# Second FFN's output kept in rows with the residual turned back to rows beforehand; attention with three PSUM banks for transposes, one bank for two accumulators, and one product for the learned tokens' values

## Chip, cores and metric

One core of one Trainium2 chip. The metric is device time in microseconds (us) of one execution. The kernel before takes 1973.4 us, the median of three runs (1972.02 to 1973.48). The engines are PE (TensorE matmul; PEld its weight loads), DVE (VectorE), ACT (ScalarE), POOL (GpSimd) and SP (SyncE, which issues most DMAs).

## What is computed

One layer of a decoder trunk on 1024 tokens of width 1024, with 16 learned tokens ahead of them, all in float32:

```python
h = h + 0.5 * swiglu(rms_norm(h, ffn1_norm), ffn1_w_in, ffn1_w_out)
u = rms_norm(h, mix_norm) @ w_in
hq, hf, hi, hg, sq, sk, sv = jnp.split(u, ...)
o_hg = hgrn2(hq, hf, hi, hg, lb, hgrn_out_norm, valid)     # gated recurrence, 4 heads
o_sb = stick_breaking(sq, sk, sv, sb_q_norm, sb_k_norm, valid)   # 8 heads of 64
h = h + concat([o_hg, o_sb]) @ w_out
h = h + 0.5 * swiglu(rms_norm(h, ffn2_norm), ffn2_w_in, ffn2_w_out)
return h[:, pad + N_META:, :]
```

`swiglu(h, w_in, w_out)` is `(silu(g) * u) @ w_out` with `g, u = split(h @ w_in)`; the inner width is 2816. In `stick_breaking` a query t weighs each earlier key s, the learned tokens among them, with `sigmoid(z_ts) * prod_{s<j<t} (1 - sigmoid(z_tj))`, and the output is the sum of weights times values.

## The kernel before

**Numbers.** Products are made of two parts of each float32 operand: a rounded high part (`wh`, `xh`, ...) and the rest (`wl`, `xl`, ...). Where three PE instructions stand together they are high by high, low by high and high by low. ACT casts the high part, DVE subtracts for the low one.

**Stages.** The first FFN runs to about 700 us; projections of queries, keys and values follow (to 870), then the attention (to 1141), the recurrence and the output projection of the mix (to 1324), and the second FFN: `fast_in` (its products with w_in, 1324 to 1748) and `fast_out` (with w_out, 1748 to the end). The activations lie transposed, features on partitions and tokens along a row (`hT`), in the FFNs.

**fast_out** multiplies 2x2 blocks in seven block products, named A12, A11, S1, S2, S4, S3, A22 after the left operand. Their sums are gathered in two groups of four PSUM banks, x and y. A finished group m is added with factor 0.5 onto the residual (`evict`, L703 on DVE). The residual `hT` was stored to DRAM as `h2D` ahead of `fast_in` and is loaded again in `fast_out` (L2347). After S3 and after A22 half of the tokens is done: `store_out` turns it back to rows, four transposes (L1065) to a bank, 32 transposes a call; ACT (L1068) or DVE (L1070) copies each bank to a row tile `orow`, and SP stores it (L1071).

**Attention.** 8 heads by 4 pairs of 128-query blocks make 32 jobs (`sb_jobs`). A job has three lists of steps: scores (`z`, L1624, L1625, L1627; ACT's sigmoids L1630 and L1631; a DVE scan L1634; POOL's product L1640), turns (the weights are transposed on PE into a bank `flip`, L1479, those of the learned tokens by L1533, and split by ACT, L1602, and DVE, L1603, to `wu` or `wm`), and values. A value step is a product with the high weights over 128 columns of v, which holds its high part in 64 columns and its low part in the other 64 (L1554), and one with the low weights over the high 64 (L1556). The last value step of a job is that of the learned tokens (`oacc<-wm,v`). Then `sb_out` copies the lower half of the accumulator (ACT, `olow`, L1595) and adds it to the upper half (DVE, `ot`, L1596).

**What sets the order.** PE's order is that of the program text (manual schedule). `braid` (L1681) lays the three lists of each job on a time grid, with lags of two jobs for the turns and three for the values, and fills in between with projections for the recurrence (`proj`, L258 to L260; their gates L1126, L1133, L1134, their weights' split L241 and L243). The other engines are ordered by a scheduler by what each instruction needs. SP issues its DMAs in queue order. PSUM has 8 banks: in the attention 2 for the fill's projections, 2 for scores (`pz`), 2 for flips (`ptr`) and 2 for accumulators (`po`, tiles `oacc`).

**Other lines of the change.** `put_split` of keys and queries (L1397) casts to `ohi`; the last of them is the kT piece of head pair 3. `fast_in` splits each weight block at L369 (ACT) and L371 (DVE), `s` being a sum of blocks made on POOL or DVE (L390) and `raw` a block as loaded; its products are `qa`, `qb`, `qc` (L458), read by DVE at L490, L541, L548 and L551. The function that turned x at the start of the kernel (L1047, tiles `xrow` and `xts`, DRAM `xD`) transposes 32x32 squares on DVE and lets the DMA place the squares.

Of the kernel before, what the change touches and what calls it, by code (L numbers as in the profile page):

```python
# [49 lines left out]
class Block:  # L50
# [308 lines left out]
    def fast_in(self, ops, n, w_in, actD, openers, ev0, open_ev, feed=None, meta=None, spare=None,  # L359
# [7 lines left out]
        def operand(src):  # L367
            hi = wp.tile([P, 4, P], F32R, tag="wh", name="wh", bufs=3)
            nc.scalar.copy(hi, src)  # L369
            lo = wp.tile([P, 4, P], F32R, tag="wl", name="wl", bufs=3)  # L370
            nc.vector.tensor_sub(lo, src, hi.bitcast(F32))  # L371
            return hi, lo
# [3 lines left out]
        def block(i, h, col):  # L376
            t = wp.tile([P, 4, P], F32, tag="raw", name="raw", bufs=self.in_bufs)
            with self.tc.issue_after(loaded[-1].ins) if loaded else ExitStack():
# [3 lines left out]
                ))  # L382
            return t
# [240 lines left out]
    def fast_out(self, hT, cs, n, w_out, actD, ready, between=lambda a, q: None,  # L624
                 meta=lambda a, q, blocks: None):
# [74 lines left out]
        def evict(bank, i, j, step, ms=range(4)):  # L700
            for m in ms:
                h = hT[:, 4 * i + m, cs[j] : cs[j] + n]
                nc.vector.scalar_tensor_tensor(  # L703
                    h, banks[bank][m], 0.5, h, ALU.mult, ALU.add
                )
            if 3 in ms:
                ready(step)
# [7 lines left out]
        for bank, a, b, start, (i, j) in steps:  # L715
# [4 lines left out]
            for q in range(nq):  # L720
# [10 lines left out]
                for m, e, at, wh, wl, xh, xl in order:  # L731
                    y, z = ((wh, xh), (wl, xh), (wh, xl))[e]
                    nc.tensor.matmul(  # L733
# [324 lines left out]
    def store_out(self, hT, pool, pps, c0, n, tag):  # L1058
        nc = self.nc
        for i, r0 in enumerate(range(c0, c0 + n, P)):  # L1060
            for q in range(2):
                row = pool.tile([P, 512], F32, tag="orow", name="orow", bufs=4)
                ps = pps.tile([P, 4, P], F32, tag=f"{tag}{(2 * i + q) % 4}", name="o")
                for k in range(4):
                    nc.tensor.transpose(ps[:, k, :], hT[:, 4 * q + k, r0 : r0 + P], self.ident)  # L1065
                dst = row.rearrange("p (k c) -> p k c", k=4)
                if q == 0:
                    nc.scalar.copy(dst, ps)  # L1068
                else:
                    nc.vector.tensor_copy(dst, ps)  # L1070
                nc.sync.dma_start(self.out[0, r0 : r0 + P, 512 * q : 512 * q + 512], row)  # L1071
# [30 lines left out]
    def hgrn_fill(self, xh, xl, pool, dst):  # L1102
# [3 lines left out]
        self.stores, self.level_banks = [], "zo"  # L1106
# [4 lines left out]
        def use(kind, h, ps, c0, n):  # L1111
# [11 lines left out]
            elif kind == "f":  # L1123
                k = staged(n)
                nc.scalar.activation(t, ps, AF.Sigmoid)
                nc.scalar.activation(k, ps, AF.Sigmoid, scale=-1.0)  # L1126
# [16 lines left out]
        def part(i, ci, c0, n, half):  # L1143
            if ci == 0 and half == 0:
                kept["w"] = self.ahead_w.pop(cols[i])
                for c in cols[i + 1 : i + (3 if i == 0 else 2)]:
# [260 lines left out]
    def sb_v(self, p, vT, mix, vD):  # L1407
# [6 lines left out]
        for c0, nb, m in ((META, 16, 32), (META + 512, 16, 32), (0, 1, META)):  # L1414
# [9 lines left out]
            for b in range(4):  # L1424
                to = vD[p, b // 2, :m, j0 : j0 + nb].rearrange(
                    "r j (i b d) -> r (j i) b d", i=2, b=2
                )
                with self.tc.issue_after(self.last_load.ins):
# [6 lines left out]
    def sb_qk(self, p, qT, kT, pool, mix, dst):  # L1435
# [31 lines left out]
        for src, c0, b0, nb in rows:  # L1467
# [4 lines left out]
            with self.tc.issue_after(self.rounds[self.columns[-1]]) if p == 3 else ExitStack():  # L1472
# [9 lines left out]
    def sb_jobs(self, keys, fetch, pool):  # L1482
# [29 lines left out]
        def job(p, hh, qs, ks, v, b0):  # L1512
# [15 lines left out]
            def meta():  # L1528
                wm.extend(kept["wm"][0])
# [4 lines left out]
                self.sb_parts([t[:META] for t in wm], ps)  # L1534
# [7 lines left out]
            def values(j):  # L1542
                if j == 0:
                    acc.append(self.po.tile([P, 256], F32, tag="o", name="oacc"))
                o = acc[0]
                if j == b0 + 2:
                    w = [t.rearrange("p b t -> p (b t)") for t in wm]
                    vj, c = v[:, 0], slice(0, 256)
                else:
# [4 lines left out]
                nc.tensor.matmul(o[:, c], vj, w[0], start=j == 0, stop=False,  # L1554
                                 skip_group_check=True)
                nc.tensor.matmul(o[:64, c], vj[:, :64], w[1], start=False, stop=end,  # L1556
                                 skip_group_check=True)
# [7 lines left out]
        kept["wm"] = [[fetch.tile([P, 2, P], F32R, name=f"wm{j}{i}") for i in range(2)]  # L1565
                      for j in range(2)]
        for t in chain(*kept["wm"]):
            nc.vector.memset(t.bitcast(F32), 0.0)
        none = kept["wm"][1][1].rearrange("p b t -> p (b t)").bitcast(F32)[META:]
        for p in range(4):  # L1570
            for a in range(4):
                to = vD[p, :, 0 if a else META :, a].rearrange("h r c -> r h c")
                nc.sync.dma_start(
                    to, none[: to.shape[0]].rearrange("r (h c) -> r h c", h=2)
# [186 lines left out]
    def run(self):  # L1761
# [21 lines left out]
        with ExitStack() as c0:  # L1783
            with ExitStack() as c1:
# [373 lines left out]
                with tc.manual_schedule(engines={nc.tensor.engine}):  # L2158
# [14 lines left out]
                    cf.close()  # L2173
                    self.proj_tags[0] = tag
# [24 lines left out]
            self.h2D = self.dram.tile([KT, P, SEQ], F32, name="h2D")  # L2199
            ph = self.pool("h2")  # L2200
# [12 lines left out]
            with tc.manual_schedule(engines={nc.tensor.engine}), ExitStack() as cx:  # L2213
# [96 lines left out]
                def after_opened():  # L2310
                    both = ph.tile([P, 16, n], F32R, tag="h2", name="parts", bufs=1)
                    self.parts = {"w": both[:, :8], "t": both[:, 8:]}

                steps = self.fast_in(
                    ops, n, a["ffn2_w_in"][0], actD, 2, ev0, open_ev, made,
                    after_opened=after_opened,
# [9 lines left out]
                drain(steps)  # L2326
            with tc.manual_schedule(engines={nc.tensor.engine}), ExitStack() as c1:
                self.ring = self.pool("ring", ctx=c1, side="right")
                hT = self.pool("h3", ctx=c1).tile([P, KT, SEQ], F32, name="hT3")
                self.op = self.pool("op", ctx=c1)  # L2330
                self.pout = self.pool("pout2", 1, PSUM, c1)
                fin = self.pool("fin", ctx=c1)

                def ready(step):
                    if step == "S3":
                        self.store_out(hT, fin, self.pout, cB, n, "y")
                    elif step == "A22":
                        self.store_out(hT, fin, self.pout, cA, n, "y")

# [35 lines left out]
```

## Time and profile before

| | us |
|---|---|
| median of 3 runs | 1973.4 (1972.02 to 1973.48) |
| profiled execution | 1973.63 |
| its span, first to last instruction or transfer | 1971.9 |
| PE busy | 1936.1 (98%) |
| DVE busy | 1390.4 (71%) |
| ACT busy | 854.9 (43%) |
| POOL busy | 445.0 (23%) |
| attention, 870 to 1141.5: PE busy | 265.09 of 271.50 |
| second FFN, fast_in, 1324 to 1748: PE busy | 422.66 of 424.00 |
| second FFN, fast_out, 1748 to 1971.9: PE busy | 217.95 of 223.90 |

The granted TensorE clock is 1.00 in all stretches but the last (0.99). A row of the timeline reads: start, duration, engine, line, operation, tile written <- tiles read, shapes, how many such in a row, and in brackets the idle time of the engine before it with what ended that. Matmuls are pipelined: a row's duration is longer than the step to the next row. A row of waits reads: engine, tile and line that waited <- engine, tile and line that released it: total us, times, longest.

### The profile page before, as it was taken

The page shows a single profiled execution, that of the slowest core. Times are in us where ns is not written, and L with a number is a line of the kernel's source. Part 1 is how long each engine was busy: PE and PEld are TensorE (multiplying, and loading weights), DVE is VectorE, ACT ScalarE, POOL GpSimd, SP SyncE. Part 2 cuts the span into 40 slices and gives each one's busy share as a digit, 9 for nine tenths or more (in the row PEclk, how much of TensorE's full clock was granted, in tenths as well). Part 3 has the DMA queues.
Part 4 walks back from the last instruction along what each step waited for, and adds up shares of the span by engine and source line. Part 5 has one row for each costly group of instructions (what it writes and reads, how often), then busy time and mean ns, then how long its engine had stood idle before and what let it go on. Part 6 is the DMA issues. An engine that isn't in the chain of part 4 may idle for free.

```text
span 1971.9 us, 30437 instructions
## 1 busy us (share of the span) xinstructions
PE 1936.1 (98%) x10768; PEld 1629.3 (83%) x10768; DVE 1390.4 (71%) x2178; ACT 854.9 (43%) x1719; POOL 445.0 (23%) x614
## 2 busy tenths in 40 slices
PE   7999999999999999999999999999999999999998
PEld 6888888888888888888898978887888888888887
DVE  7977777877678665467777666667577766767764
ACT  6523343334444544366666635433223333344443
POOL 3010100001000003133333342210545544620000
PEclk9999999999999999999999999999999999999999
DMA  7356787758966325765454178646433323378463
GB/s 210 93 164 169 250 272 240 243 192 299 371 217 189 117 61 149 178 181 146 126 148 118 58 248 244 161 184 203 160 106 108 108 94 104 102 281 295 123 193 139
DMA packets 346362, 347.17 MB, mean 176 GB/s; under 512 B 94993, under 2 KB 250513, under 8 KB 346209
## 3 DMA queue, kind: packets, MB, share of 16 engines
q1 hardware_dynamic: 325360, 283.73, 47.1%
q0 software_dynamic: 19808, 61.49, 9.0%
q8 instruction: 85, 1.39, 0.3%
q14 instruction: 69, 0.56, 0.1%
q10 hardware_dynamic: 1040, 0.00, 0.0%
HBM read 233.75 MB, written 111.38 MB: 175 GB/s over the span
## 4 chain that ended last, share of the span: by engine, by line
PE 73%; issue 16%; DVE 4%; DMA 2%; POOL 2%; ACT 2%; SPq 1%; POOLq 0%; DVEq 0%; ACTq 0%
PE o L733 21%; PE qb L458 11%; PE qa L458 8%; PE qc L458 7%; PE proj L258 4%; PE proj L260 4%; PE proj L259 4%; PE flip L1479 2%; PE wo L259 1%; PE wo L258 1%; PE wo L260 1%; PE oacc L1554 1%; PE oacc L1556 1%; PE z L1624 1%; DMA KB<-hg_k 1%
## 5 line engine op out<-in xcount | busy, mean ns | idle before, releaser
L458 PE MATMUL qb<-T,wh 128*128 128x512 f32 x1056 | 344.4, 390 | 1.3 <-ACT T L318 0.8
L458 PEld LDWEIGHTS qb<-T,wh 128*128 128x128 f32 x1056 | 198.1, 188 | 46.1 <-issue 2.5
L458 PE MATMUL qa<-B,wh 128*128 128x512 f32 x696 | 226.8, 391 | 0.0
L258 PE MATMUL proj<-xh,wh 128*128 128x512 f32 (+2 forms) x640 | 213.4, 333 | 2.4 <-ACT st L1126 1.3
L733 PE MATMUL o<-t,w 128*128 128x512 f32 x924 | 212.2, 390 | 0.6 <-DVE u L551 0.5
L260 PE MATMUL proj<-xl,wh 128*128 128x512 f32 (+2 forms) x640 | 209.8, 328 | 0.8 <-DVE xl L1948 0.8
L733 PE MATMUL o<-parts 128*128 128x512 f32 x924 | 209.9, 389 | 0.0
L259 PE MATMUL proj<-xh,wl 128*128 128x512 f32 (+2 forms) x640 | 209.8, 328 | 0.0
L458 PE MATMUL qb<-T,wl 128*128 128x512 f32 x528 | 205.5, 389 | 0.0
L733 PEld LDWEIGHTS o<-t,w 128*128 128x128 f32 x924 | 172.7, 188 | 37.8 <-issue 0.8
L733 PEld LDWEIGHTS o<-parts 128*128 128x128 f32 x924 | 173.3, 188 | 36.0
L371 DVE TENSOR_TENSOR wl<-s,wh 128x512 fp32r<-128x512 f32 x160 | 165.7, 1035 | 50.8 <-ACT wh L369 49.8
L369 ACT CAST wh<-s 128x512 fp32r<-128x512 f32 x160 | 99.4, 622 | 194.1 <-PE qb L458 146.1
L458 PEld LDWEIGHTS qa<-B,wh 128*128 128x128 f32 x696 | 130.7, 188 | 27.3 <-DVE B L837 0.3
L369 ACT CAST wh<-raw 128x512 fp32r<-128x512 f32 x120 | 74.4, 621 | 148.0 <-PE qc L458 108.0
L458 PE MATMUL qa<-B,wl 128*128 128x512 f32 x348 | 135.6, 390 | 0.0
L258 PEld LDWEIGHTS proj<-xh,wh 128*128 128x128 f32 x640 | 120.6, 188 | 14.4 <-ACT st L1126 1.9
L260 PEld LDWEIGHTS proj<-xl,wh 128*128 128x128 f32 x640 | 120.4, 188 | 12.1 <-DVE xl L1948 1.2
L259 PEld LDWEIGHTS proj<-xh,wl 128*128 128x128 f32 x640 | 120.5, 188 | 9.9
L458 PE MATMUL qc<-T,wh 128*128 128x512 f32 x352 | 117.1, 394 | 0.0
L458 PE MATMUL qc<-B,wh 128*128 128x512 f32 x352 | 115.0, 390 | 1.4 <-DVE u L551 1.4
L458 PEld LDWEIGHTS qb<-T,wl 128*128 128x128 f32 x528 | 99.1, 188 | 20.3
(399 smaller groups left out, 3865.6 us busy)
## 6 DMA issues: line engine op xcount, KB each, us to landing
raw<-in_ffn_w_in_dram SPq DMA_DIRECT2D x176, 256.0 KB, 4.1
raw<-in_ffn_w_out_dram SPq DMA_DIRECT2D x112, 256.0 KB, 4.3
w2in<-both SPq DMA_DIRECT2D x28, 512.0 KB, 3.4
raw<-in_w_in_dram SPq DMA_DIRECT2D x25, 512.0 KB, 5.2
ks<-kD SPq DMA_DIRECT2D x32, 260.0 KB, 4.8
wout<-both SPq DMA_DIRECT2D x16, 512.0 KB, 3.8
wh<-w2in SPq DMA_DIRECT2D x27, 256.0 KB, 3.3
wl<-w2in SPq DMA_DIRECT2D x27, 256.0 KB, 3.2
```

What stands on the lines that cost most here:

```text
L258: nc.tensor.matmul(ps, wh[:, s], xs, start=k == 0, stop=False)
L259: nc.tensor.matmul(ps, wl[:, s], xs, start=False, stop=False)
L260: nc.tensor.matmul(ps, wh[:, s], xl[:, k, c0 : c0 + n], start=False, stop=k == nk - 1)
L369: nc.scalar.copy(hi, src)
L371: nc.vector.tensor_sub(lo, src, hi.bitcast(F32))
L458: nc.tensor.matmul(ps, a[:, k, :], b[:, k, :], start=start and k == 0 and i == 0, stop=k == 3 and i == 2, skip_group_check=True,)
L733: nc.tensor.matmul(banks[bank][m], y[:, m * P : (m + 1) * P], z, start=start and at == 0 and e == 0, stop=q == nq - 1 and e == 2, skip_gro ...
L1479: self.nc.tensor.transpose(ps[:m, j, :], src[:, s0 : s0 + m], self.ident)
L1554: nc.tensor.matmul(o[:, c], vj, w[0], start=j == 0, stop=False, skip_group_check=True)
L1556: nc.tensor.matmul(o[:64, c], vj[:, :64], w[1], start=False, stop=end, skip_group_check=True)
L1624: nc.tensor.matmul(z, q, ks[0][:, s0 : s0 + n], start=True, stop=False)
```

## The change

- **Second FFN's output in rows.** `fast_out` gets `rows=True`: the two operands of each product change places, so a bank holds 128 tokens by 512 features, and `evict` adds it onto `hR`, the residual in rows. After each final addition the 128x512 piece is stored straight away, from POOL's queue for A11, S4 and S3 (12 stores), from SP's for A22 (4). `store_out` is gone: its 64 transposes, 16 copies and 16 stores.
- **The residual turned back.** A new generator `turn_back` runs in `fast_in`: it loads each of 16 pieces 128x512 of `h2D` (`hcol`), transposes its 32x32 squares on DVE (`hrow`) behind a low part `wl<-s`, and stores it with four DMAs to `h2R`, which lies in rows. `fast_out` loads `hR` from it.
- **Attention.** `ptr` has 3 banks and `po` 1. The two accumulators are the halves `both[:, 0]` and `both[:, 1]` of one tile of one bank, used in turn. `wm` holds the learned tokens' high weights in rows 0 to 15 and their low ones in rows 32 to 47; `vD` gets the values' high part a second time at rows 32 to 47, so one product (L1592 of the changed kernel) does what two did.
- **Smaller moves.** The last kT piece's cast waits for the first gate's second sigmoid instead of a projection round, and the fill asks for one column of weights less ahead.

The core of the diff:

```diff
         def evict(bank, i, j, step, ms=range(4)):
             for m in ms:
-                h = hT[:, 4 * i + m, cs[j] : cs[j] + n]
+                h = (hT[:, 4 * j + m, 512 * i : 512 * i + 512] if rows
+                     else hT[:, 4 * i + m, cs[j] : cs[j] + n])
                 nc.vector.scalar_tensor_tensor(
                     h, banks[bank][m], 0.5, h, ALU.mult, ALU.add
                 )
+                if rows and step in ("A11", "S4", "S3", "A22"):
+                    r0 = n * j + P * m
+                    eng = nc.sync if step == "A22" else nc.gpsimd
+                    eng.dma_start(self.out[0, r0 : r0 + P, 512 * i : 512 * i + 512], h)
...
                     y, z = ((wh, xh), (wl, xh), (wh, xl))[e]
+                    if rows:
+                        y, z = z, y
...
-    def store_out(self, hT, pool, pps, c0, n, tag):
...
+    def turn_back(self, pool, src, dst):
...
+            with tc.issue_after(self.block_load.ins):
+                nc.sync.dma_start(t, src[m, :, 512 * half : 512 * half + 512])
...
+            for b in range(4):
+                c0 = P * m + 32 * b
+                with tc.issue_after(self.block_load.ins):
+                    nc.sync.dma_start(
+                        dst[512 * half : 512 * half + 512, c0 : c0 + 32]
+                        .rearrange("(f j) d -> j f d", j=32),
+                        t[32 * b : 32 * b + 32].rearrange("j (f d) -> j f d", d=32),
+                    )
...
+            with tc.issue_after(self.block_lo.ins):
+                nc.vector.transpose(t, cols)
...
                 if j == 0:
-                    acc.append(self.po.tile([P, 256], F32, tag="o", name="oacc"))
+                    if "oacc" not in kept:
+                        both = self.po.tile([P, 2, 256], F32, name="oacc")
+                        kept["oacc"] = [both[:, 0], both[:, 1]]
+                    acc.append(kept["oacc"][0])
+                    kept["oacc"].reverse()
...
-                nc.tensor.matmul(o[:, c], vj, w[0], start=j == 0, stop=False,
+                nc.tensor.matmul(o[:, c], vj, w[0], start=j == 0, stop=end,
                                  skip_group_check=True)
-                nc.tensor.matmul(o[:64, c], vj[:, :64], w[1], start=False, stop=end,
-                                 skip_group_check=True)
-                if end:
+                if not end:
+                    nc.tensor.matmul(o[:64, c], vj[:, :64], w[1], start=False, stop=False,
+                                     skip_group_check=True)
+                else:
                     self.sb_out(p, hh, b0, o, kept, pool, oD)
...
-                    self.ptr = self.pool("ptr", 2, PSUM, c1)
-                    self.po = self.pool("po", 2, PSUM, c1)
...
+                        self.ptr = self.pool("ptr", 3, PSUM, c2)
+                        self.po = self.pool("po", 1, PSUM, c2)
...
+                    self.ptr = self.pool("ptr1", 2, PSUM, c1)
+                    self.po = self.pool("po1", 2, PSUM, c1)
```

On PE nothing else moves: 32 products and 64 transposes are gone. The place where one job ends and the next one's values begin, before the change (the second of 31 such boundaries; numbers behind names tell tiles apart; the last bracket is what the row waits for, named after the engine whose count it awaits):

```order
L1533 MATMUL flip_8923<-ident_65,sig_8682 16x128 [waits DVE_49]
L1533 MATMUL flip_8923<-ident_65,sig_8714 16x128
L1554 MATMUL oacc_8850<-wm10_7908,v_7939 128x256 [waits Activation_49]
L1556 MATMUL oacc_8850<-wm11_7909,v_7939 64x256
L1554 MATMUL oacc_8933<-wu_8855,v_7939 128x256 [waits Activation_49]
L1556 MATMUL oacc_8933<-wu_8856,v_7939 64x256 [waits DVE_49]
L1624 MATMUL z_8939<-ks_8667,qs_8666 128x456 [waits PE_49]
L1625 MATMUL z_8939<-ks_8668,qs_8666 128x456
```

And in the changed kernel:

```order
L1568 MATMUL flip_8937<-ident_65,sig_8698 16x128 [waits DVE_49]
L1568 MATMUL flip_8937<-ident_65,sig_8730 16x128
L1592 MATMUL oacc_8770<-wm1_7909,v_7941 128x256 [waits Activation_49]
L1592 MATMUL oacc_8770<-wu_8869,v_7941 128x256 [waits DVE_49]
L1595 MATMUL oacc_8770<-wu_8870,v_7941 64x256
L1663 MATMUL z_8951<-ks_8683,qs_8682 128x456 [waits PE_49]
L1664 MATMUL z_8951<-ks_8684,qs_8682 128x456
```

The second product of the learned tokens is gone, both jobs write the one tile `oacc_8770`, and the first value product of the next job awaits DVE, where it awaited ACT: the count is that of the addition `ot<-oacc,olow` (L1596; L1635 of the changed kernel) of the job whose last product stands in the row above. So it is at all 31 boundaries.

On DVE in the second FFN's `fast_in`, before:

```order
L490 TENSOR_TENSOR u_15077<-qb,p_15016 128x512
L371 TENSOR_TENSOR wl<-s,wh 128x512
L551 TENSOR_TENSOR u<-qc,u_15077 128x512
L371 TENSOR_TENSOR wl<-raw,wh 128x512
L552 TENSOR_TENSOR sg<-u,sg 128x512
L551 TENSOR_TENSOR u<-qb,p_15016 128x512
```

The same place in the changed kernel:

```order
L491 TENSOR_TENSOR u_15044<-qb,p_14983 128x512
L371 TENSOR_TENSOR wl<-s,wh 128x512
L1092 STREAM_TRANSPOSE hrow<-hcol 128x512
L552 TENSOR_TENSOR u<-qc,u_15044 128x512
L371 TENSOR_TENSOR wl<-raw,wh 128x512
L553 TENSOR_TENSOR sg<-u,sg 128x512
L552 TENSOR_TENSOR u<-qb,p_14983 128x512
```

A transposition has come between a low part and the reading of a product's bank; there are 16 such places.

On SP at the end of the program, before:

```order
L642 DMA raw<-in_ffn_w_out_dram 128x512
L1071 DMA out_dram<-orow 128x512 x4
L642 DMA raw<-in_ffn_w_out_dram 128x512
L1071 DMA out_dram<-orow 128x512 x3
L647 DMA act<-act9T_12651 128x512
L642 DMA raw<-in_ffn_w_out_dram 128x512
L647 DMA act<-act10T_12658 128x512
L1071 DMA out_dram<-orow 128x512 x8
```

And in the changed kernel:

```order
L643 DMA raw<-in_ffn_w_out_dram 128x512
L648 DMA act<-act8T_12606 128x512
L643 DMA raw<-in_ffn_w_out_dram 128x512 x2
L648 DMA act<-act9T_12613 128x512
L648 DMA act<-act10T_12620 128x512
L643 DMA raw<-in_ffn_w_out_dram 128x512
L711 DMA out_dram<-hR 128x512 x4
```

The stores between the last loads are gone from SP; twelve of the sixteen stores now stand at the end of POOL's order, behind all its other work.

More of the change, by code (lines that the diff above doesn't have):

```diff
@@ L1056, in turn_x, with load, store @@
             yield
[L1058 to L1071 removed]
+    def turn_back(self, pool, src, dst):
+        nc, tc = self.nc, self.tc
+        places = [(m, half) for half in range(2) for m in range(KT)]
+        def load(i):
+            m, half = places[i]
+            t = pool.tile([P, 512], F32, tag="hcol", name="hcol", bufs=2)
+            with tc.issue_after(self.block_load.ins):
+                nc.sync.dma_start(t, src[m, :, 512 * half : 512 * half + 512])
+            return t
+        def store(t, m, half):
+            for b in range(4):
[6 more added lines that the diff above has]
+                    )
+        cols = load(0)
+        yield
+        for i, place in enumerate(places):
+            t = pool.tile([P, 512], F32, tag="hrow", name="hrow", bufs=2)
+            with tc.issue_after(self.block_lo.ins):
+                nc.vector.transpose(t, cols)
+            if i + 1 < len(places):
+                cols = load(i + 1)
+            yield
+            store(t, *place)
     def proj_bank(self, n):
```

78 lines of the change are left out of this document (47 added, 31 removed).

## The prediction

> **What bounds the kernel now.** I read the page's busy times first, then the busy time by stage, then the waits of the stage with the attention, and last the timeline at the places where the diff touches PE.
>
> ```profile
> PE 1936.1 (98%) x10768; PEld 1629.3 (83%) x10768; DVE 1390.4 (71%) x2178; ACT 854.9 (43%) x1719; POOL 445.0 (23%) x614
> ```
>
> By stage (columns: the stretch, its length, then busy time of PE, PEld, DVE, ACT and POOL, the granted clock, the DMA share and GB/s):
>
> ```profile
> 870.00:1141.50 271.50, 265.09 (x1884) 236.71 (x1883) 194.73 (x318) 174.36 (x447) 96.29 (x136) 1.00 0.43 121
> ...
> 1324.00:1748.00 424.00, 422.66 (x1862) 347.08 (x1861) 294.48 (x339) 134.60 (x227) 186.12 (x186) 1.00 0.38 124
> 1748.00:1971.90 223.90, 217.95 (x993) 180.79 (x991) 145.96 (x231) 88.17 (x154) 7.96 (x9) 0.99 0.63 212
> ```
>
> PE is busy in 98% of the span and in 265.09 of 271.50 us of the attention, 422.66 of 424.00 of the second FFN's first half and 217.95 of 223.90 of its second. So PE bounds all three stages that the change touches: a product that goes is worth its own step on PE, and a wait put into PE's queue costs all of itself. DVE and ACT have room, so what is added there costs only if PE comes to wait for it.
>
> **Terms that go.** (1) The learned tokens' low-half products: one of L1556 per job, 32 in all.
>
> ```profile
> 958.52 0.36 PE L1554 MATMUL oacc<-wm,v 128*128 128x256 f32 x1
> 958.72 0.29 PE L1556 MATMUL oacc<-wm,v 128*64 128x256 f32 x1
> 958.85 0.28 PE L1554 MATMUL oacc<-wu,v 128*128 128x256 f32 x1
> 959.19 0.37 ACT L1595 COPY olow<-oacc 64x256 f32<-64x256 f32 x1
> 959.64 0.42 DVE L1596 TENSOR_TENSOR ot<-oacc,olow 64x256 f32<-64x256 f32 x1
> ```
>
> One lasts 0.29 us, but the next product starts 958.85 − 958.72 = 0.13 us later, and that step is what PE gets back; over several boundaries it is 0.12. 32 × 0.12 = **−3.8 us**.
>
> (2) The transposes of the output, 32 after S3 and 32 after A22 (L1065), with their copies (L1068 on ACT, L1070 on DVE).
>
> ```profile
> 1926.80 2.48 DVE L703 SCALAR_TENSOR_TENSOR hT<-o,hT 128x512 f32<-128x512 f32 x4
> ...
> 1928.29 4.10 PE L1065 MATMUL o<-ident,hT 128*128 128x128 f32 x32
> ...
> 1932.14 30.22 PE L733 MATMUL o<-parts 128*128 128x512 f32 x132
> ...
> 1960.35 2.74 DVE L703 SCALAR_TENSOR_TENSOR hT<-o,hT 128x512 f32<-128x512 f32 x4 [7.12 <-PE o L733]
> ...
> 1962.20 3.90 PE L1065 MATMUL o<-ident,hT 128*128 128x128 f32 x32
> ...
> 1967.65 0.69 DVE L1070 COPY orow<-o 128x512 f32<-128x512 f32 x1 [0.56 <-DMA out_dram<-orow]
> ```
>
> After S3 the 32 transposes start at 1928.29 and A22's products at 1932.14: 3.85 us. What is late next is A22's first product into bank x0, which adds to what S3's eviction reads. That eviction takes 2.48/4 = 0.62 us a bank from 1926.80 and has left x0 by 1927.4 and x3 by 1929.3, while A22 reaches x3 only after three quarters of its first 12 products, at about 1930.3. So all of it is won: **−3.9**. At the end, the last add ends at 1960.35 + 2.74 = 1963.09. Now it is followed by transposes and copies, whose last ends at 1967.65 + 0.69 = 1968.34; the span ends 3.56 us later, for the store. With the change a 256 KB store hangs on the add itself: 1963.09 + 3.56 = 1966.65 against 1971.9, **−5.2**.
>
> (3) Three banks for flips instead of two. The waits of PE between 870 and 1141.5 us:
>
> ```profile
> PE flip L1479 <- DVE wu L1603: 2.9, 7, 0.7
> PE flip L1479 <- DVE wm L1603: 1.5, 3, 0.6
> PE proj L258 <- DVE st L1134: 0.7, 1, 0.7
> ```
>
> A flip waits for a bank that DVE still reads: 2.9 + 1.5 = **−4.4** if the third bank takes all of it. The bounds are 0 and the whole idle time of the stretch, 271.50 − 265.09 = −6.4.
>
> (4) The last keys' split stands behind two gate sigmoids. What it can win is the wait of the first product after it:
>
> ```profile
> 855.95 0.39 PE L258 MATMUL proj<-xh,wh 128*128 128x256 f32 x1 [1.28 <-ACT st L1126]
> ```
>
> Between 0 and −1.3; I take **−0.6**, as ACT has the same work in another order.
>
> **The term that comes.** The third bank is taken from the accumulators. There were two tiles oacc, each with a bank; now there is one tile with two halves in one bank. The order on PE shows what follows: at all 31 boundaries between jobs the first value product of the next job waits for DVE's add `ot<-oacc,olow` (L1596) of the job just ended, where before it wrote the other bank and waited for at most an older cast on ACT. The halves do not overlap, but the wait is there. Behind the waiting product stand, on PE's one queue, the next scores, flips and fill projections; ACT's sigmoids and DVE's scans wait for those, so all shift together.
>
> The chain is: last product of the job, ACT's copy olow, DVE's add ot, release, product. The profile of before has each link; here once with both engines idle, and once with work queued ahead:
>
> ```profile
> 1037.24 0.28 PE L1556 MATMUL oacc<-wm,v 128*64 128x256 f32 x1
> 1037.56 0.37 ACT L1595 COPY olow<-oacc 64x256 f32<-64x256 f32 x1 [1.04 <-PE oacc L1556]
> ...
> 1037.96 0.41 DVE L1596 TENSOR_TENSOR ot<-oacc,olow 64x256 f32<-64x256 f32 x1 [0.78 <-ACT olow L1595]
> ```
>
> ```profile
> 995.12 0.60 ACT L1133 ACTIVATE st<-proj 128x512 f32<-128x512 f32 x1 [2.32 <-PE proj L260]
> ...
> 995.38 0.29 PE L1556 MATMUL oacc<-wm,v 128*64 128x256 f32 x1
> ...
> 995.51 0.28 PE L1554 MATMUL oacc<-wu,v 128*128 128x256 f32 x1
> ...
> 995.62 1.04 ACT L241 CAST wh<-raw 128x1024 fp32r<-128x1024 f32 x1
> ...
> 996.93 0.37 ACT L1595 COPY olow<-oacc 64x256 f32<-64x256 f32 x1
> ...
> 998.27 0.42 DVE L1596 TENSOR_TENSOR ot<-oacc,olow 64x256 f32<-64x256 f32 x1
> ```
>
> At 1037.24 both engines were idle and waiting: the add ends at 1038.37, 1.13 us after the product's start; with 0.06 for a release (between the 0.03 from olow to ot here and the 0.08 at 959.56) 1.19, the shortest of all. At 958.72 it ends at 960.06 and the next job's product started 0.13 us after the meta product: a stall of 1.27 with the release. At 995.38 ACT had a gate and a 1.04 us cast ahead of olow, and DVE a lo split ahead of ot: the add ends at 998.69, the next product would have run at 995.51, a stall of 3.24. Other boundaries have PE work between the two products, which covers part:
>
> ```profile
> 968.35 0.28 PE L1556 MATMUL oacc<-wm,v 128*64 128x256 f32 x1
> ...
> 968.91 0.36 PE L1554 MATMUL oacc<-wu,v 128*128 128x256 f32 x1
> ...
> 969.29 0.42 DVE L1596 TENSOR_TENSOR ot<-oacc,olow 64x256 f32<-64x256 f32 x1
> ```
>
> Here four products lie between, 0.56 us, and the stall is 969.71 + 0.06 − 968.91 = 0.85. I did the same for all 31 (the rows are these 32 pairs, first and last start in them):
>
> ```profile
> L1595 ACT COPY olow<-oacc x32: 367/367/370, 884.0 to 1140.6; 64x256 f32<-64x256 f32 x32
> ...
> L1596 DVE TENSOR_TENSOR ot<-oacc,olow x32: 415/417/420, 884.9 to 1141.0; 64x256 f32<-64x256 f32 x32
> ```
>
> By products between: none, 8 boundaries, 14.5 us; two, 1 boundary, 1.8; four, 10, 12.2; seven, 6, 8.2; sixteen, 5, 3.8; nineteen, 1, 0. Sum 40.4, from 0.4 to 3.2 each. That keeps ACT's and DVE's queues as they are and is the upper end. The lower end takes the shortest chain, 1.19, everywhere, less the cover of 0.12, 0.26, 0.57 and 0.85: 8 × 1.07 + 0.93 + 10 × 0.62 + 6 × 0.34 = 17.7. What stands ahead of olow and ot are gates and casts that PE's own work released just before, as at 995.12, and a stalled PE doesn't call them off; but each stall lets both engines work off a little. I take **+35**, nearer to the observed.
>
> [...]
>
> **Costed at nothing.** The second FFN's first half gets 16 transposes on DVE and 80 small DMAs on SP.
>
> ```profile
> L371 DVE TENSOR_TENSOR wl<-s,wh 128x512 fp32r<-128x512 f32 x72 | 105.4, 1464 | 40.6 <-ACT wh L369 39.9
> ...
> L490 DVE TENSOR_TENSOR u<-qb,p 128x512 f32<-128x512 f32 x44 | 30.2, 686 | 26.4 <-PE qb L458 26.4
> ...
> L551 DVE TENSOR_TENSOR u<-qc,u 128x512 f32<-128x512 f32 x21 | 14.5, 691 | 22.0 <-PE qc L458 22.0
> ```
>
> ```profile
> L1047 DVE STREAM_TRANSPOSE xts<-xrow x16: 701/704/712, 112.5 to 352.5; 128x512 f32<-128x512 f32 x16
> ```
>
> ```profile
> xD<-xts SPq DMA_DIRECT2D x64, 64.0 KB, 3.9
> ```
>
> The same transposition runs in the first FFN at 0.70 us; beside POOL it could take as long as a split there, 1.46. 16 × 0.70 to 16 × 1.46 = 11 to 23 us enter an engine that is idle 424 − 294 = 130 us of this stage and waits 26.4 and 22.0 us of it for PE. So 0, with +3 as a bound where a transpose stands ahead of a late split. The 64 small stores have their like in the 64 of the first FFN (3.9 us to landing), and the rows they make are needed only from 1748 on. Fill zeros and the doubled low rows for vD are SP work before 870, POOL takes 12 output stores from SP; neither has an instruction of PE waiting.
>
> **The sum.** −3.8 − 3.9 − 5.2 − 4.4 − 0.6 + 35 = +17.1, on the profiled execution's own 1973.63 us: 1990.7. It lies 0.2 above the median of 1973.4, so I forecast **1990.5 us**.
>
> **Rivals.** *The wait is covered (faster).* At the boundaries with sixteen products between, the stall is 0.4 where the add isn't late; if jobs, once stretched, settled so that olow and ot ran at once and in cover, the stalls would fall. They decide at 17.9 us, the sum of the gains: the lower end is 17.7, so the change is faster only if the stalls lie under the shortest chain of the trace, or the wait is released otherwise than I read it. With no stall at all the time is 1973.4 − 17.9 = 1955.5. Against it: the wait stands in PE's order 31 times, and eight times nothing lies between. Chance 0.08.
>
> *About even.* Stalls at the shortest chain, 18 to 22 us: 1970 to 1977. It needs ACT's and DVE's queues empty at every boundary; at 995.38 they were not. 0.06.
>
> *The second FFN's first half goes over to DVE.* If each transpose held a split that PE needs, up to 23 us come on top: 1990.5 + 23 = 2013. Against it, 130 us of idle DVE. 0.05.
>
> *Third bank without effect.* The flips wait for DVE's read, not for a bank count that a stalled PE has anyway: term (3) is 0, and 1990.5 + 4.4 = 1995. 0.2, inside the range of slower, with my forecast itself at 0.61.
>
> **How the numbers follow.** Low end of my case: 17.7 − 6.4 − 3.8 − 9.1 − 1.3 = −2.9, all bounds at once, 1970.5; high: 40.4 − 3.8 − 9.1 + 3 = +30.5, 2004. I give 1975 to 2003, which leaves out the faster case, most of the transposes' case and a part of the even one, some 0.17. A measurement of this kernel can tell 0.2%, 3.9 us, from no change. Faster 0.08, same 0.06, slower 0.86.
>
> **What would show it.** In the attention: waits of `oacc` for DVE `ot` about 31 times, 1 us on average, the stretch 870 to 1141 longer by some 27 us, and no more flip waits. In the second FFN: the first half at 424 us as now, the second shorter by about 9, its end an add and 3.6 us. If value products wait for nothing, or for ACT alone, the main term is wrong, and the time falls below 1960; if `qb` or `qc` wait for a `wl`, the transposes were not free.

## The result

The changed kernel takes 2006.54 us (median of four runs, 2004.66 to 2008.35), the kernel before 1973.44 (1972.02 to 1974.78): a ratio of 1.0167, 95% interval 1.0152 to 1.0183. It is slower by 33.1 us, where 17 were forecast and the range ended at 2003. The profiled execution took 2005.66 us with a span of 2003.9, 32.0 us over that of before. One execution of e5 below, 3244.45 us at a mean clock of 0.557, is left out of e5's figures.

The busy time by stage in the changed kernel (columns as in the prediction; the attention's stretch runs from its first value product to its last, and the last two stretches are the halves of the second FFN):

```profile
877.16:1182.80 305.64, 266.42 (x1822) 235.28 (x1821) 197.48 (x308) 172.68 (x435) 91.82 (x133) 0.98 0.37 105
1366.00:1790.00 424.00, 422.66 (x1862) 347.10 (x1861) 298.78 (x356) 134.77 (x226) 186.59 (x185) 1.00 0.47 144
1790.00:2003.90 213.90, 210.11 (x927) 173.63 (x926) 140.03 (x223) 83.88 (x146) 14.31 (x21) 1.00 0.65 221
```

The same stretch of the attention before:

```profile
875.16:1140.60 265.44, 259.51 (x1854) 232.22 (x1853) 189.36 (x308) 170.65 (x435) 91.66 (x133) 1.00 0.43 120
```

The attention is 40.2 us longer. PE's idle time there rose from 5.9 to 39.2 us, and its busy time rose too, from 259.5 to 266.4, although 32 products are gone: look at the granted clock, 0.98 where it was 1.00. The second FFN did what was forecast: its first half takes 424 us as before, its second is shorter by about 10. Two smaller pieces are left: the projections ahead of the attention end 2.0 us later than before, and all else is within 0.5 us.

PE's waits in the changed kernel, all program long and longest first (engine, tile, line <- releaser: us, times, longest):

```profile
PE oacc L1592 <- DVE ot L1635: 38.4, 30, 3.3
...
PE proj L258 <- ACT st L1151: 3.0, 1, 3.0
```

The first row is the wait that the prediction set against the gains, at 30 of 31 boundaries; the flips' 4.4 us are gone. The last is a wait of the projections ahead of the attention for a gate's sigmoid; before, PE waited 1.3 us for one there.

Two boundaries of the changed kernel, a short stall and the longest, which answer to those of 958.72 and 995.38:

```profile
974.34 0.36 PE L1592 MATMUL oacc<-wm,v 128*128 128x256 f32 x1
...
974.62 0.36 ACT L1641 CAST wm<-flip 16x256 fp32r<-16x256 f32 x1 [2.46 <-PE flip L1568]
...
975.01 0.37 ACT L1634 COPY olow<-oacc 64x256 f32<-64x256 f32 x1
975.46 0.42 DVE L1635 TENSOR_TENSOR ot<-oacc,olow 64x256 f32<-64x256 f32 x1
...
975.93 0.39 PE L1592 MATMUL oacc<-wu,v 128*128 128x256 f32 x1 [1.23 <-DVE ot L1635]
```

```profile
1016.65 0.60 ACT L1159 ACTIVATE st<-proj 128x512 f32<-128x512 f32 x1 [2.32 <-PE proj L260]
1016.71 0.36 PE L1592 MATMUL oacc<-wm,v 128*128 128x256 f32 x1
1017.15 1.04 ACT L241 CAST wh<-raw 128x1024 fp32r<-128x1024 f32 x1
...
1018.22 1.22 DVE L243 TENSOR_TENSOR wl<-raw,wh 128x1024 fp32r<-128x1024 f32 x1 [0.24 <-ACT wh L241]
1018.47 0.37 ACT L1634 COPY olow<-oacc 64x256 f32<-64x256 f32 x1
...
1019.92 0.42 DVE L1635 TENSOR_TENSOR ot<-oacc,olow 64x256 f32<-64x256 f32 x1
...
1020.39 0.58 PE L1592 MATMUL oacc<-wu,v 128*128 128x256 f32 x1 [3.31 <-DVE ot L1635]
```

The product starts 0.05 us after the add's end each time (975.88 and 975.93, 1020.34 and 1020.39). At 1016.65 the same gate, cast and split stand ahead of the copy and the add as at 995.12 in the kernel before: they were released by PE work that ran before the stall. From the last product of one job to the first of the next it takes 3.68 us, and that first product lasts 0.58 where the other lasts 0.39. The granted clock (last but two of each row) around this place shows why:

```profile
1016.00:1020.00 4.00, 1.08 (x8) 0.77 (x6) 2.41 (x4) 2.15 (x4) 0.00 (x0) 1.00 0.17 68
1020.00:1022.00 2.00, 1.61 (x6) 1.19 (x7) 0.34 (x1) 0.41 (x1) 0.73 (x1) 0.53 0.65 179
1022.00:1024.00 2.00, 2.00 (x13) 2.00 (x12) 1.17 (x2) 1.47 (x3) 0.00 (x0) 0.61 0.66 214
1024.00:1028.00 4.00, 4.00 (x34) 3.83 (x34) 1.97 (x3) 1.98 (x5) 0.55 (x1) 1.00 0.00 0
```

Behind the stall the clock is halved for 3.4 us (0.47 x 2 + 0.39 x 2 = 1.72 us lost). This happens five times in the profiled execution: at 859.7, behind the gate's wait, and at 917.7, 948.5, 1006.5 and 1020.1. That is 5 x 1.7 = 8.5 us, worked out from the granted clock. Before, the clock is 1.00 from 17 us to the last few.

The end, on DVE and SP: four adds, a store behind each, and 3.1 us from the last add's end, 2000.84, to the span's end.

```profile
1998.11 2.73 DVE L705 SCALAR_TENSOR_TENSOR hR<-o,hR 128x512 f32<-128x512 f32 x4 [7.11 <-PE o L741]
1998.83 2.37 SPq L711 DMA_DIRECT2D out_dram<-hR  x4
```

### The profile page after: what moved, and what is told of

It reads as the page before. It is cut to its first block, busy times and chain, and to the rows that moved or that the text cites. A ratio compares the mean times of both kernels' runs of the same rounds, so it can differ in the third digit from the quotient of the medians.

```text
span 2003.9 us, 30415 instructions
## 1 busy us (share of the span) xinstructions
PE 1935.8 (97%) x10672; PEld 1626.6 (81%) x10672; DVE 1396.5 (70%) x2184; ACT 854.3 (43%) x1711; POOL 453.8 (23%) x626
## 5 line engine op out<-in xcount | busy, mean ns | idle before, releaser
L1679 POOL TENSOR_TENSOR sig<-sig,keep 128x144 f32<-128x144 f32 (+3 forms) x64 | 80.9, 1265 | 181.4 <-DVE keep L1673 107.0
```

The lines of the kernel that those rows point to most:

```text
L1679: nc.gpsimd.tensor_mul(sig, sig, keep[:, 1 : nk + 1])
```

## The experiments

Theory A, formed on these traces: the loss is the wait for the shared bank (43.7 us over 31 boundaries, as the step from the product before to the next job's first value product, less 0.12; 38.4 of it idle, the rest the restart), the halved clock that the longer stalls bring, and a gate that became late. Theory B is the prediction as it stood: 35 us of stall, no price of the clock.

**e1: the bank part undone.**

```diff
-                    if "oacc" not in kept:
-                        both = self.po.tile([P, 2, 256], F32, name="oacc")
-                        kept["oacc"] = [both[:, 0], both[:, 1]]
-                    acc.append(kept["oacc"][0])
-                    kept["oacc"].reverse()
+                    acc.append(self.po.tile([P, 256], F32, tag="o", name="oacc"))
...
-                        self.ptr = self.pool("ptr", 3, PSUM, c2)
-                        self.po = self.pool("po", 1, PSUM, c2)
+                        self.ptr = self.pool("ptr", 2, PSUM, c2)
+                        self.po = self.pool("po", 2, PSUM, c2)
```

> The changed kernel with the bank part undone: two accumulator tiles in banks of their own and two banks for flips; rows output, single product for the learned tokens and the small moves stay. Theory A (the shared bank costs its stalls, 43.7 us over 31 boundaries in the trace of the changed kernel, and four halvings of the granted clock, 4 x 1.7 us): 2006.5 - 43.7 - 6.8 + about 6 for the flips that wait again = 1962 us, granted clock 1.00 from 870 us on, one halving left near 860 us. Theory B (the prediction's sizes: 35 us of stall and no cost of the clock, the rest of the loss lies elsewhere in the change): 2006.5 - 35 + 4.4 = 1976 us.

1963.08 us against 1974.71 beside it (ratio 0.9946, 0.9931 to 0.9961). The waits of the attention and the projections ahead of it:

```profile
PE flip L1514 <- DVE wu L1638: 4.4, 9, 0.8
PE proj L258 <- ACT st L1151: 3.0, 1, 3.0
...
PE oacc L1591 <- DVE wu L1638: 0.7, 2, 0.5
PE proj L258 <- DVE st L1160: 0.7, 1, 0.7
PE flip L1514 <- DVE wm L1638: 0.6, 1, 0.6
```

Its attention:

```profile
878.40:1142.90 264.50, 256.25 (x1821) 228.53 (x1820) 196.14 (x308) 170.71 (x435) 91.31 (x130) 1.00 0.42 121
```

The gain of 11.6 us agrees with theory A's 1962 and not with B's 1976. No product waits for `ot`, flips wait again, and the clock is halved once only, for twice 3.4 us on end behind the 3.0 us of the gate (0.89 on average from 840 to 870 us, 1.00 from 870 to 1184). Net of all that it brings, the shared bank costs some 43 us (2006.54 - 1963.08).

**e2: the bank part alone**, the same edit on the kernel before, the other way round.

> The kernel before with the bank part alone: one tile with two halves for the accumulators, three banks for flips. Theory A: 1973.4 + 43.7 + 6.8 - 6 = 2018 us, with several halvings of the clock in the attention. Theory B: 1973.4 + 35 - 4.4 = 2004 us, clock 1.00.

2016.89 us against 1974.71 (1.0222, 1.0206 to 1.0238). The attention of this kernel:

```profile
874.90:1182.20 307.30, 272.52 (x1854) 240.49 (x1852) 190.43 (x308) 172.58 (x435) 92.34 (x133) 0.97 0.37 104
```

It grows by 41.9 us with the clock at 0.97, without any other part of the change. B is 13 us off. A's 2018 comes within 1.1 us, but two of its sizes make up for each other: the stalls sum to 38.6 us by A's measure, not 43.7, and the clock is halved for seven times 3.4 us, six of them in the attention, not for four.

**e3: the second FFN's rows alone**, on the kernel before.

> The kernel before with the second FFN's output in rows alone. Both theories: the whole gain of the second FFN, 9.7 us by the trace of the changed kernel (9.1 by the prediction): 1963.7 to 1964.3 us, the first half of that FFN at 424 us as before. If the 16 transposes or the 80 small transfers cost something that the attention hides in the comparison of the two traces: up to 23 us more, so 1965 to 1987.

1963.73 us against 1974.71 (0.9951, 0.9935 to 0.9968): 11 us by these medians, where 9.7 were expected. By the trace the span is 10.9 us shorter, 9.5 of it in the second FFN's second half; the rest lies ahead of that FFN, which starts 1.5 us sooner. Attention and the second FFN's halves:

```profile
873.90:1139.30 265.40, 259.42 (x1854) 232.23 (x1853) 189.54 (x308) 170.81 (x435) 91.56 (x133) 1.00 0.42 120
1323.00:1747.00 424.00, 422.66 (x1862) 347.17 (x1861) 299.61 (x356) 134.56 (x226) 186.00 (x186) 1.00 0.48 144
1747.00:1961.00 214.00, 209.87 (x926) 173.49 (x925) 140.10 (x222) 83.69 (x146) 14.77 (x21) 1.00 0.64 220
```

The first half takes 424 us as before, so the 16 transposes and 80 small transfers cost PE nothing. Beside e1, whose attention takes 264.5 us with the single product, 265.4 here says that the 32 removed products are worth 0.9 us there and not 3.8: PE is busy for 3.2 us less in e1 (256.25 against 259.42) and idle for 2.3 more, of which the flips' waits are 0.5 (5.0 us in e1, 4.5 in e3). What the rest of the idle time is stays open, and e1 has the added vD stores and the smaller moves besides.

**e4: the stalls kept, PE kept busy in them.**

```diff
+                    n = WARM[kept["job"]]
+                    kept["job"] += 1
+                    if n:
+                        d = self.ptr.tile([P, 512], F32, tag="tr", name="warm")
+                        for _ in range(n):
+                            nc.tensor.matmul(d, v[:, 0], v[:, 0:4].rearrange("p a b -> p (a b)"),
+                                             start=True, stop=True)
                 o = acc[0]
```

> The changed kernel with idle products added in the stalls: ahead of each job's first value product PE runs 2 to 13 products of 512 columns into a bank of the flips that nothing reads, so many as end before the wait does by the trace. Nothing of the output changes. [...] Rival (the halved clock only accompanies the stalls and costs nothing by itself): 2006.5 or more, since nothing else gets faster.

By theory A the stalls stay and the four halvings in the attention go: 2006.5 - 6.8 = 2000 us.

1998.18 us against 1974.71 (1.0124, 1.0109 to 1.0140), 8 us faster than the changed kernel with 130 products more. Its attention and the wait that is left of the stalls:

```profile
876.40:1175.80 299.40, 290.55 (x1952) 251.44 (x1950) 197.40 (x308) 172.51 (x435) 91.97 (x133) 1.00 0.38 107
```

```profile
PE oacc L1600 <- DVE ot L1643: 7.9, 28, 0.4
```

The clock is 1.00, and the stretch is 6.2 us shorter than the changed kernel's 305.6. So the halved clock has a price of its own, and it can be had back with work that does nothing. In this execution the gate's wait, 2.8 us, brought no halving either, though no idle product stands there; so 6.2 of the 8 us are the idle products' doing, where four halvings had been put at 6.8.

**e6: the bank shared, the order changed.** The third lag of the braid is that of the values.

```diff
+                pack = 0.75 if lag == value else 1.0
                 for t, f in steps:
-                    waiting.append((at + lag + (done + t / 2) / total, t, f))
+                    waiting.append((at + lag + pack * (done + t / 2) / total, t, f))
```

> The changed kernel, one bank for both accumulators and three for flips, with only the grid of the braid altered: the value steps of a job are laid in the first three quarters of its slot, so that 10 to 30 rows of other work stand on PE between the last value product of a job and the first of the next at 27 of the 31 boundaries (2 or 6 at the others, where they were 0 to 18). Theory A (the cost is the distance in PE's order, shorter than the chain of copy, add and release): stalls of some 8 us remain of 43.7, and no halving: 1973.4 - 9.7 - 3.8 - 4.4 + 8 + 2.4 = 1966 us. Rival (sharing the bank costs by itself, through the engines' accesses to it, wherever the products stand): above 1990.

1966.67 us against 1972.69 (0.9967, 0.9954 to 0.9980), where the changed kernel's ratio is 1.0167. The longest of the waits left in the attention:

```profile
PE oacc L1592 <- DVE ot L1635: 6.9, 6, 3.0
```

What costs is the distance in PE's order: the shared bank is still there, and 6.9 us of its waits are left of 38.4. Two halvings that theory A had not expected are in this trace, one behind the gate (860.0) and one behind the longest of these waits (1068.2); that the time came out at A's 1966 all the same is in part luck. No cost of sharing by itself shows: e11 below, in which no product waits for the add, is faster than every kernel here with two accumulator banks.

**e7: two flip banks beside the shared accumulators** (`ptr` from 3 to 2).

> The changed kernel with two banks for flips again, the accumulators still in one (a bank lies idle): what the third bank is worth beside the stalls. The prediction's term: 4.4 us slower than the changed kernel, 2011. Rival of the prediction (third bank without effect, since PE stalls anyway): 2006.5.

2005.05 us against 1972.69 (1.0161, 1.0145 to 1.0176), no different from the changed kernel. The attention's longest wait, and that of the flips:

```profile
PE oacc L1592 <- DVE ot L1635: 38.0, 30, 3.3
...
PE flip L1568 <- DVE wu L1642: 0.2, 1, 0.2
```

With two banks the flips wait 0.2 us. In the changed kernel the third bank brought nothing, as the rival had it. That a stalled PE comes to the flips late enough anyway fits this, with PE's waits for the add at 38.0 us here and 38.4 there.

**e5, e8, e9: the late gate.** First the added vD stores on POOL's queue, in the changed kernel (e5) and in the two-bank kernel (e8):

```diff
-                        nc.sync.dma_start(
+                        nc.gpsimd.dma_start(
                             vD[p, b // 2, :m, 1, 32 * (b % 2) : 32 * (b % 2) + 32],
```

> The changed kernel with the 16 added small stores of the values' high part (vD) issued from POOL's queue instead of SP's; all else as changed. Theory A (a gate waits 3.0 us at 859 us because the store hg_v that frees its buffer stands on SP behind these small stores, and the clock is halved once behind it): the wait and the halving there go, 2006.5 - 3.0 - 1.7 = 2002 us. Rival (the wait comes from the gate's move ahead of the last key cast): no change, 2006.5.

> Rows output, the learned tokens' single product, two banks each for flips and accumulators, and the added vD stores on POOL's queue. From the two-bank kernel's 1963.1 less the late gate (3.0 of wait, up to 3.4 of halved clock): 1958 to 1960 us. If the gate is late for another reason: 1963.

e5 took 2005.58 us (1.0162, 1.0145 to 1.0179) and e8 1964.36 (0.9956, 0.9940 to 0.9973), both against 1972.69: no gain. The gate's wait in e5 and in e8, with no halving near it in e8 (1.0 on average over the execution):

```profile
PE proj L258 <- ACT st L1151: 3.2, 2, 1.9
```

```profile
PE proj L258 <- ACT st L1151: 2.8, 2, 1.7
```

In e5 the clock is still halved once there, from 864.9 to 868.3. The store of hg_v did go out 3.4 us earlier (853.12 in e5, 856.56 in the changed kernel), and the wait behind it is 1.3 us, but a second one came after it. Its cause is in e5's trace: the gate stands on ACT behind the cast of the next weights, and that cast waits for their load.

```profile
861.27 1.04 ACT L241 CAST wh<-raw 128x1024 fp32r<-128x1024 f32 x1 [3.29 <-DMA raw<-in_w_in_dram]
...
862.78 0.38 ACT L1151 ACTIVATE st<-proj 128x256 f32<-128x256 f32 x1
...
863.22 0.50 PE L258 MATMUL proj<-xh,wh 128*128 128x512 f32 x1 [1.85 <-ACT st L1151]
```

The change asks for one column of weights less ahead, which fits a late load. Then e9, the two-bank kernel with the smaller moves undone and the stores on SP:

> The two-bank kernel of before (rows output, single product, two banks each) with the smaller moves undone: the last key cast and the first weight cast stand ahead of the gates again, and the fill asks for two columns ahead. The added vD stores stay on SP. Theory A (after the run with the stores on POOL: the late gate comes from the move, not from the stores): PE waits near 857 us fall from 3.0 us or more to 1.3 and the clock stays 1.00: 1963.1 - 1.7 - up to 1.7 = 1960 to 1961.5 us. Rival (the added stores on SP hold hg_v here too): waits of 3 us, 1963.

1963.54 us against 1972.89 (0.9951, 0.9939 to 0.9964), and the wait is

```profile
PE proj L258 <- ACT st L1151: 2.4, 2, 1.3
```

Theory A's 1960 to 1961.5 us did not come. With neither the added stores nor the moves (e3, and the kernel before) the wait is 1.3. So the moves, with the added stores on POOL, make PE's waits for the gate 1.5 to 1.9 us longer (e8, e5), the stores on SP without the moves 1.1 (e9: the second wait follows the store of hg_v), and both together 1.7. So the two don't add up: in the changed kernel ACT's cast waits 2.12 us for its weights at 861.35, but no product waits behind it. What either is worth in the time is open: the medians of e1, e8 and e9 lie within 1.3 us.

**e10 and e11: what the experiments point to.** Shared accumulators, three flip banks, rows output, single product, smaller moves undone, value steps packed into 0.6 and 0.5 of the slot.

> One accumulator bank and three flip banks, value steps in the first 0.6 of a job's slot, smaller moves undone: 14 or more rows between jobs at 27 of 31 boundaries, 6 or 8 at the rest. Theory A (a shared bank is free where the next job's products stand further off than the chain of 1.3 to 3.7 us, and three banks then save the flips' waits): stalls of 3 us or less are left, no flip waits, no halving: 1963.7 (rows alone) - 3.8 - 5 + 3 = 1958 us. Rival (denser value steps make PE wait for the split weights instead): 1963 or more.

> As e10 with the value steps in the first half of the slot: 16 or more rows at all boundaries. Theory A: no stall for the add, 1956 to 1958 us. Rival (denser value steps run ahead of the split weights or of the flips): slower than e10.

1957.98 us (0.9923, 0.9909 to 0.9936) and 1957.82 us (0.9924, 0.9912 to 0.9936), both against 1972.89. e10's attention, and the longest waits there and in the projections ahead of it (of the 2.9 us, 0.2 are in the attention):

```profile
875.20:1136.40 261.20, 255.67 (x1828) 229.53 (x1827) 196.78 (x310) 171.76 (x441) 93.60 (x134) 1.00 0.44 123
```

```profile
PE oacc L1588 <- DVE ot L1631: 3.7, 3, 1.4
PE proj L258 <- ACT st L1151: 2.9, 3, 1.4
```

The change with its bank plan beats both kernels once the order gives the add its time: 4.2 us of the attention are won where 40.2 were lost. In e11 no product waits for `ot`, but 1.8 us are waited for `wu`, and the time is the same.

## Why the prediction was wrong

By its own steps, on the span, 1971.9 to 2003.9:

| step | forecast | measured |
|---|---|---|
| stalls at the boundaries | +35 | +43.7 |
| halved clock | none | +8.5 (5 x 1.7, from the granted clock) |
| gate and projections ahead of the attention, without the halving | -0.6 | +0.3 (2.0 - 1.7) |
| single product | -3.8 | -3.8 (32 x 0.12, taken over) |
| flips and other waits in the attention | -4.4 | -6.5, what is then left of the attention's 40.2; not by the third bank (e7) |
| second FFN | -9.1 | -9.7 |
| the rest | 0 | -0.5 |

**The direction and the mechanism were right.** The shared bank is the loss (e1, e2), the wait is the one named, at 30 of 31 boundaries, and it is the distance in PE's order that prices it (e6, e10). The second FFN's terms were right, the transposes were free (e3).

**The step that failed first** is "but each stall lets both engines work off a little. I take +35". The walk over the boundaries had given 40.4 from the rows of before, and 43.7 came. Nothing was worked off: what stands ahead of the copy and the add was released by PE before the stall, so its length is the same (the rows at 1016.65 repeat those at 995.12). Taken one by one, 29 of the 31 stalls are as long as the walk's to 0.02 us, or longer.

Nor was the walk's sum an upper end, as the prediction had called it. The walk was made on the kernel with two products of the learned tokens, and e2, which keeps both, bears it out: where no product lies between, its eight stalls are the walk's to 0.01 us. In the changed kernel these eight are 0.19 to 0.35 us longer. ACT has its cast of `wm` ahead of the copy (974.62 above), so the copy starts 0.67 us after the first of the learned tokens' products in both kernels (958.52 to 959.19, 974.34 to 975.01), while PE, with one product less, is at the wait sooner. By theory A's measure the stalls are 43.7 us with one product and 38.6 with two, so what the single product takes out of PE's work came back as longer stalls.

**The step that was missing** is the granted clock. The prediction read it as 1.00 in all stretches and asked no more, though its own list had stalls of over 3 us. It is about a quarter of the loss, 8.5 of 32.0; e4, with the four halvings in the attention gone, gets back 6.2 us of the attention. Either miss alone would have left the time within the range, 1990.5 + 8.7 = 1999.2 or 1990.5 + 8.5 = 1999.0; the two together did not.

**The small moves** were costed at -0.6, and the vD stores at nothing, on the ground that no instruction of PE waits for them. One does, at one remove. The gate's buffer is freed by the store of hg_v, and that stands on SP behind the added stores:

```profile
854.58 1.93 SPq L1461 DMA_DIRECT2D vD<-vhl  x1
...
856.56 0.42 SPq L1146 DMA_DIRECT2D hg_v<-st  x1
```

```profile
858.84 0.39 ACT L1151 ACTIVATE st<-proj 128x264 f32<-128x264 f32 x1 [4.62 <-DMA hg_v<-st]
```

```profile
859.29 0.39 PE L258 MATMUL proj<-xh,wh 128*128 128x256 f32 x1 [3.00 <-ACT st L1151]
```

The move did take away the wait of 1.28 that it was credited with, and a later one of 3.00 took its place. With the stores away from SP it is the weights' load that comes late (e5), so by these traces both small parts hold up the gate.

**The third bank** was the rival that came true: no effect where PE stalls (e7). That the term's size came near, -4.4 for -6.5, is luck. With the stalls nearly gone and three flip banks, e10's attention is 3.3 us shorter than that of e1 with two (261.2 against 264.5 us); but the order differs too, and no run has three flip banks and two for accumulators, so the third bank's own share is not shown.

Whether the two halves need the wait between them no run tests, for none leaves it out. What the runs show is the wait's price: here two halves of one bank do the work of two banks only where the order keeps their users apart. The changed kernel waits 38.4 us for the add and takes 2006.54 us; e6 waits 6.9 and takes 1966.67, e10 waits 3.7 and takes 1957.98, with two banks e1 takes 1963.08.

## What to carry to other kernels

Before two accumulators are laid into one bank, or any buffer count is lowered, count the rows on the bounding engine between the last use of one and the first of the next, and walk the release chain with the other engines' queues as they stand; don't discount it. Then add the clock: behind five of the nine stalls of more than 1.5 us in the changed kernel it was halved for 3.41 us, some 1.7 us lost each time. And if the chain can't be shortened, an order that puts other work between the two uses takes the stall away: here +33 us became -6 by one factor in the grid that sets the order (e6), and -15 with a smaller factor and the small moves undone (e10).

## What the runs showed of the hardware

**Behind some stalls of PE the granted clock was halved for 3.41 us.** In the profiled execution of the changed kernel PE is idle for more than 1.5 us nine times between its first product and its last. The table has the starts of the products on both sides (us), the step between them, the part of it that PE is idle, and the stretch at a clock of 0.50 that followed:

| last product | next product | step | idle | clock 0.50 |
|---|---|---|---|---|
| 856.01 | 859.29 | 3.27 | 3.00 | 859.71 to 863.12 |
| 893.61 | 895.59 | 1.98 | 1.61 | none |
| 913.54 | 916.60 | 3.07 | 2.79 | 917.74 to 921.15 |
| 945.77 | 948.00 | 2.24 | 1.97 | 948.46 to 951.87 |
| 1003.92 | 1006.11 | 2.19 | 1.91 | 1006.49 to 1009.90 |
| 1016.71 | 1020.39 | 3.68 | 3.31 | 1020.14 to 1023.55 |
| 1093.29 | 1096.81 | 3.52 | 3.15 | none |
| 1169.14 | 1171.12 | 1.98 | 1.62 | none |
| 1179.15 | 1181.06 | 1.90 | 1.63 | none |

Each stretch lasts 3.41 us, so it costs 1.7 us where PE is busy through it (an estimate, 3.41 x 0.50). In the last of the five the clock fell 0.25 us before the next product's start, in the others up to 1.14 us after it. From 1023.55 to 2003.18 us it is 1.00.

The length of the stall alone does not tell whether a halving follows. The step of 3.52 us from 1093.29 to 1096.81 has none:

```profile
1092.00:1096.00 4.00, 1.66 (x16) 1.38 (x14) 3.25 (x5) 3.14 (x7) 0.00 (x0) 1.00 0.81 219
1096.00:1100.00 4.00, 3.19 (x18) 2.60 (x19) 2.16 (x4) 1.88 (x4) 1.50 (x3) 1.00 0.25 72
```

In e5 the same boundary has the same step of 3.5 us (1091.24 to 1094.75), and there the clock is halved:

```profile
1090.20:1093.60 3.40, 1.40 (x13) 1.12 (x12) 2.94 (x4) 2.88 (x7) 0.00 (x0) 1.00 0.79 208
1093.60:1097.00 3.40, 2.25 (x10) 1.82 (x10) 1.04 (x3) 0.84 (x2) 1.50 (x3) 0.50 0.27 92
```

And the step of 2.24 us from 945.77 to 948.00 in the changed kernel has one:

```profile
946.00:948.00 2.00, 0.04 (x1) 0.00 (x0) 1.94 (x6) 1.29 (x5) 0.00 (x0) 1.00 0.58 168
948.00:950.00 2.00, 2.00 (x9) 1.66 (x10) 1.63 (x3) 0.94 (x4) 1.53 (x2) 0.61 0.60 207
```

So 1.91 us of idle time were followed by a halving and 3.15 were not; what decides it, these runs do not show. The four runs of the changed kernel had spans of 2003.0, 2003.9, 2005.7 and 2006.6 us at mean clocks of 0.997, 0.996, 0.996 and 0.994, the shortest with the highest clock and the longest with the lowest; where the halvings fell in three of them is not on record.
